# Second pass of a bidirectional DeltaNet layer: which ScalarE and VectorE work may overtake the copies of the triangular inverse

## The chip, the cores and the metric

The kernel runs on one core of a Trainium2 chip. The metric is the device time of one execution in microseconds, on that core. A core has a matmul engine (TensorE, PE in the profile), a vector engine (VectorE, DVE), an activation engine (ScalarE, ACT), a general engine (GpSimd, POOL) and a queue that issues the loads and stores (SyncE, SP). Each works through a list of its own, and they wait for each other by semaphores.

## The reference, cut to what matters

One layer is computed for 128 context tokens and 2048 latent tokens of width 1024: a modulated norm, one input projection, a DeltaNet branch in both directions beside a gated MLP branch, one output projection, and then a squared-ReLU MLP of width 4096 with a final norm. The part that matters here is the DeltaNet scan, in chunks:

```python
decay = where(incl, exp(where(incl, diff, 0.0)), 0.0)      # from the cumulated gates
a_mat = where(strict, einsum(k_beta, k) * decay, 0.0)
sol = triangular_solve(a_mat + eye, rhs, lower=True, unit_diagonal=True)
...
def step(S, xs):
    v_new = u_c - w_c @ S
    o = qd @ S + qk_c @ v_new
    S = S * exp(gl) + kd.T @ v_new
    return S, o
```

It runs once forwards and once backwards over the tokens. The two outputs are added, normed, gated, put through the output projection, added to the input, and normed again for the MLP.

## The kernel before, in words

The program has three stages one after the other: the projections in token blocks (to about 436 us), the two scan passes (about 436 to 1235 us), and the MLP in a seven-product scheme per 2x2 block (from 1237.4 us, the first MLP matmul).

**Units.** The scan works in tiles of 128 tokens. There are 34 units: units 0 to 16 are the forward pass, units 17 to 33 the backward one (`d = 1`), which is called the second pass here. A unit has 17 `prep` steps and 4 `scan` steps, for all four heads at once.

- Step 0 makes the decays: `E = exp(-|g_i - g_j|)`, four ScalarE operations (line 1052) and one exponential (1053), then two masks on GpSimd (`Es`, line 1055, and `E`, line 1057).
- Step 1 makes the matrix: `KK` times beta times `Es` (VectorE, 1067, inside the helper `calm`), its diagonal on GpSimd (1071), its fp16 copy `AH` (ScalarE, 1074) and the first approximate inverse `X = AH * bd2` (VectorE, 1075).
- Step 2 transposes `X` into `Y` (matmuls of line 1081, copy of line 1083) and makes the rest `AL` (VectorE, 1084).
- Steps 3 to 12 are the levels 2, 4, 8, 16, 32: at each the inverse of blocks of twice the size is made from the smaller ones. Each has two steps: matmuls of line 1101 and a masking multiplication on VectorE (`P`, line 1105, the *mask*); then matmuls of lines 1114 and 1116 and two copies on ScalarE (`Y`, line 1117, and `X`, line 1118, the *level copies*).
- Steps 13 and 14 are the last level: matmuls of line 1133 and a ScalarE copy (1134); then matmuls of 1140 and 1142 and two copies, `Y` on VectorE (1143) and `X` on ScalarE (1144). This is the *64-join*.
- Step 15 makes the residual `R` (matmuls of 1150 and 1151, VectorE 1153), step 16 the corrected inverse `T` (ScalarE, 1162).
- The four scan steps: `vt` and the first part of the output from the state (1174, 1166); `vs` and `vn` (1187, 1189); the new state `S`, four VectorE operations (1201); the output (1215 to 1221).

**What fills the matmul engine.** In the second pass the 17 units are filled up with the output of the layer: `o_steps` norms the scan's output (`norm`, 1350 to 1358, ScalarE squares, VectorE sums and products, a power on GpSimd), transposes it and splits it into high and low parts (`trans`, 1371, `oH` 1374 on ScalarE, `oL` 1375 on VectorE), and projects it (`proj`, lines 241 to 243 in the helper `mm3`, then 1394 and 1395). For tiles over 8, `h2_steps` makes the operands of the MLP: squares (868), norm (876, 183, 184), scaling (881), transposes (888, 891), and seven operands `opH`, `opL` (903, 904).

**Order.** Every step has a due time in units of one scan unit. Steps are written out sorted by it, and the place in this order is a priority. The framework then plans each engine's list in a simulated timeline: an instruction whose inputs are there by that timeline may be placed ahead of one that was written earlier but still waits. On the chip the lists are fixed.

Two helpers limit this. `level_done(s)` notes the last instruction written as the latest urgent one of its engine (masks on VectorE, level copies on ScalarE). `calm(f, lag)` writes `f` and forbids each of its instructions to be placed ahead of the latest (`lag` = 0), the last but one (1) or the last but two (2) urgent instruction noted so far on its engine. It adds no wait on a semaphore, only an order within one engine. Before the change it is used, in the second pass, for `KK` (lag 1), for `x = x + tmp` in `proj`, and for the seven operands (`st[5:]`).

The due times in the second pass (`WINDOWS`, last ten values): prep steps of unit i lie from i - 2.63 to i + 0.06, 0.158 apart, so that three units are in work at any time; the scan steps lie at i - 0.03, i + 0.26, i + 0.56 and i + 0.85. The 64-join of unit i + 1 is due at i + 0.664.

Of the kernel before, what the change touches and what calls it, by code (L numbers as in the profile page):

```python
# [12 lines left out]
AF = mybir.ActivationFunctionType  # L13
ALU = mybir.AluOpType
# [7 lines left out]
NT = 17  # L22
NTOK = NT * P
H = 4
# [40 lines left out]
def hybrid_step(  # L65
# [7 lines left out]
    V, A, G, T = nc.vector, nc.scalar, nc.gpsimd, nc.tensor  # L73
# [52 lines left out]
    bd2 = cp.tile([P, P], F16, name="bd2")  # L126
# [21 lines left out]
    def bc4(ap):  # L148
        return ap.unsqueeze(1).to_broadcast([P, 4, P])
# [6 lines left out]
    gcol = cp.tile([P, NT, 8], F32, name="gcol")  # L156
    neg2 = cp.tile([P, NT, 8], F32, name="neg2")
    eglg = cp.tile([P, NT, 8], F32, name="eglg")
    egl = cp.tile([P, NT, 8], F32, name="egl")
# [51 lines left out]
    def here():  # L211
        return len(tc.nc.cur_bb.bb.instructions)
# [82 lines left out]
    with ExitStack() as ph:  # L295
# [17 lines left out]
        for d in range(2):  # L313
            m = p1.tile([P, P], F32, tag=f"mcum{d}", name=f"mcum{d}", bufs=1)
            s = 1 if d == 0 else -1
# [473 lines left out]
        decay = decay_steps()  # L789
        prev = None  # L790
        side = []
        for bi in range(len(BLOCKS)):
# [6 lines left out]
            at = {e: n for n, e in enumerate(order)}  # L799
            tile_of = {}  # L800
            for n, (gi, h) in enumerate(order):
                u = us[n] if bi == 0 and n < 3 else feature_tile(blk, bi, gi, h)
# [157 lines left out]
    with ExitStack() as ph:  # L960
# [8 lines left out]
        def pd():  # L969
            return psd.tile([P, 4, P], F32, tag="d", name="pd", bufs=4)  # L970
# [7 lines left out]
        def f16(tag, bufs=1):  # L978
            return pp.tile([P, 4, P], F16, tag=tag, name=tag, bufs=bufs)

        def q32(tag, bufs=1, pool=None):
            return (pool or dl).tile([P, 4, P], F32, tag=tag, name=tag, bufs=bufs)

        def s32(name):
            return pp.tile([P, 4, P], F32, tag="e", name=name, bufs=NE)
# [16 lines left out]
        def level_done(n):  # L1002

            x = tc.nc.cur_bb.bb.instructions[-1]
            urgent[x.engine].append(x)

        def calm(f, lag=0):

            start = here()
            f()  # L1010
            for x in tc.nc.cur_bb.bb.instructions[start:]:
                if x.engine in urgent and len(urgent[x.engine]) > lag:
                    tc.add_manual_dep(x, urgent[x.engine][-1 - lag].name, mybir.DependencyInfo(
                        mybir.DependencyClass.NoSync, mybir.DependencyReason.DATA), reason="order")

        def unit(t, d):

            u = {}
            sg = 1 if d == 0 else -1

            def col(tab, h):
                return tab[:, t, d * 4 + h : d * 4 + h + 1]

            def quad(p, lhs, rhs):
                for h in range(H):
                    T.matmul(p[:, h, :], lhs[:, h, :], rhs[:, h, :], start=True, stop=True)  # L1026
# [19 lines left out]
            scan = []  # L1046

            @prep.append
            def _():
                e = s32("E")  # L1050
                for h in range(H):
                    A.activation(e[:, h, :], u["gb"][:, h, :], AF.Abs, scale=-1.0, bias=col(gcol, h))
                A.activation(e, e, AF.Exp, scale=-1.0)
                es = s32("Es")
                G.affine_select(out=es, in_=e, pattern=[[0, 4], [-sg, P]], compare_op=ALU.is_gt, fill=0.0,
                                base=0, channel_multiplier=sg)
                G.affine_select(out=e, in_=e, pattern=[[0, 4], [sg, P]], compare_op=ALU.is_ge, fill=0.0,
                                base=0, channel_multiplier=-sg)
                u["Es"], u["E"] = es, e

            @prep.append
            def _():
                a = u["KK"]

                def decayed():
                    for h in range(H):
                        V.scalar_tensor_tensor(out=a[:, h, :], in0=a[:, h, :], scalar=col(beta, h),  # L1067
                                               in1=u["Es"][:, h, :], op0=ALU.mult, op1=ALU.mult)

                calm(decayed, 1) if d else decayed()  # L1070
                G.affine_select(out=a, in_=a, pattern=[[0, 4], [1, P]], compare_op=ALU.not_equal, fill=1.0,
                                base=0, channel_multiplier=-1)
                u["AH"], u["AL"], u["X"] = f16("AH", BA), f16("AL", BA), f16("X", BX)
                A.copy(u["AH"], a)
                V.tensor_tensor(out=u["X"], in0=u["AH"], in1=bc4(bd2), op=ALU.mult)

            @prep.append
            def _():
# [57 lines left out]
            @prep.append  # L1136
            def _():
                p = pd()
                for h in range(H):
                    T.matmul(p[:, h, 0:64], u["X"][:, h, :], pms[64][:, h, rb], start=True, stop=True)  # L1140
                for h in range(H):
                    T.matmul(p[:, h, 64:P], pms[64][:, h, :], u["X"][:, h, ra], start=True, stop=True)
                V.tensor_copy(u["Y"][ra, :, rb], p[ra, :, 0:64])
                A.copy(u["X"][rb, :, ra], p[rb, :, 64:P])

            @prep.append
# [44 lines left out]
            @scan.append  # L1191
            def _():
                s = u["s"]
                p = pd()
                quad(p, u["kt"], u["vs"])
                sn = q32("S", 2)
                if s is None:
                    A.copy(sn, p)
                else:
                    for h in range(H):  # L1200
                        V.scalar_tensor_tensor(out=sn[:, h, :], in0=s[:, h, :], scalar=col(egl, h),
                                               in1=p[:, h, :], op0=ALU.mult, op1=ALU.add)
                u["sn"] = sn

            @scan.append
# [205 lines left out]
        def at(time, fn, kind=None):  # L1411
            events.append((time, len(events), fn, kind))

        def spread(t0, t1, steps, kind):
            for j, st in enumerate(steps):
                at(t0 + (t1 - t0) * (j + 0.5) / len(steps), st, kind)

        def scan_step(i, f):
            def g():
                u = units[i]  # L1420
                if "s" not in u:
                    u["s"] = None if i in (0, NT) else units[i - 1]["sn"] if i not in (1, NT + 1) else u["s0"]
                f()
            return g
# [12 lines left out]
        def noted(name, f):  # L1437

            start = here()
            f()  # L1440
            done[name] = tc.nc.cur_bb.bb.instructions[start:]
# [8 lines left out]
        p2, p3 = WINDOWS[:8], WINDOWS[8:]  # L1450
        for i, u in enumerate(units):
            w = p2 if i <= NT else p3
            at(i - 3 if i > 1 else -12.1, lambda i=i, u=u: noted(("kk", i), u["prep_loads"]))
            at(i - 3 if i > 1 else -11.1, lambda i=i, u=u: after_weights(
                u["qk_load"], (("kk", 1),) if i < 2 else (), (mybir.EngineType.SP,)))
            at(i - 1, lambda i=i, u=u: after_weights(u["scan_loads"], LATER.get(i, ()), (mybir.EngineType.SP,)))
            u["prep"][:2] = [lambda i=i, f=f: after_weights(f, AHEAD_OF.get(i, ()), (mybir.EngineType.Activation,
                                                                                    mybir.EngineType.DVE))
                             for f in u["prep"][:2]]
            n = len(u["prep"])  # L1460
            for j, st in enumerate(u["prep"]):
                at(i - w[0] + (j + 0.5) * (w[0] - w[1]) / n if i or j > 9 else -11.6 if j < 2
                   else 0.2 * j - 8.15, st, "prep")
            spread(i + w[2], i + w[3], [scan_step(i, f) for f in u["scan"]], "chain")
            if i in (0, NT):
                at(i - 1, lambda i=i: state_load(i))
                at(i + w[2] + (w[3] - w[2]) * 0.7, lambda i=i: after(i))
            if i >= NT:
                at(i, lambda u=u: o_loads(u))
                first, second = o_steps(u)  # L1470
                spread(i + p3[4], i + p3[5], first, "fill")
                spread(i + p3[6], i + p3[7], second, "fill")
                if u["t"] > 8:
                    st = h2_steps(u["t"], pj, fraw, w512, fpart, fhalf, lambda u=u: u["x2"])
                    spread(i + p3[8], i + p3[9] + 0.2, st[:5], "fill")
                    spread(i + p3[9] + 0.2, i + p3[9] + 2.1, [lambda f=f: calm(f) for f in st[5:]], None)
        f2 = [f2_steps(t) for t in range(NT)]
        flat = []
# [13 lines left out]
        for j, st in enumerate(flat[:NF]):  # L1492
            g, k = divmod(j, KT + 1)
            if g == 1 and k == KT:
                st = lambda st=st: after_weights(st, AHEAD_OF[0], engines)
            if j == HT * (KT + 1):
                st = lambda st=st: after_weights(st, (("u", 4),), (mybir.EngineType.SP,))
# [457 lines left out]
    for j, t in enumerate(range(8, -1, -1)):  # L1955
        st = h2_steps(t, bank, lambda: w512("junk"), w512)
        p = 10 + 19 * j // 2
# [7 lines left out]
    for p, (o, n, b) in enumerate(seq):  # L1965
        u = units[n]
# [11 lines left out]
        e = p - last  # L1978
# [15 lines left out]
    for m, (n, i, u, q) in enumerate(todo):  # L1994
# [14 lines left out]
        h, lo = sops.pop(m)  # L2009
# [87 lines left out]
```

## Time and profile before

| | |
|---|---|
| median of 3 runs | 2576.61 us (2570.27 to 2578.84) |
| the profiled execution | 2574.76 us, of which the span of instructions is 2573.0 us |
| PE busy | 2536.3 us (99%) |
| DVE busy | 1830.8 us (71%) |
| ACT busy | 1260.1 us (49%) |
| POOL busy | 229.3 us (9%) |
| stretch 520 to 870 us (forward pass) | PE busy 347.70 of 350 us, DVE 245.45, ACT 188.89 |
| stretch 870 to 1215 us (second pass) | PE busy 330.40 of 345 us, DVE 276.22, ACT 224.03 |

Rows of a timeline give start, duration, engine, line, operation, the tiles and, in brackets, how long the engine stood idle before and what ended that. A matmul's duration runs past the start of the next one, since they are pipelined. A row of waits gives who waited for whom, the sum in us, how often, and the longest. A row of windows gives the busy time of the five engines in a stretch, then the granted clock of the matmul engine, the share of the DMA engines and GB/s.

### The profile page before, as it was taken

What the parts mean: (1) busy time and instruction counts of PE and PEld (TensorE: products, weight loads), DVE (VectorE), ACT (ScalarE), POOL (GpSimd) and SP (SyncE); (2) the same over time, 40 slices, a digit from 0 to 9 for tenths busy, and PEclk for the clock granted to TensorE, in tenths of its full rate; (3) what the DMA queues carried; (4) which work ended last, traced back from release to release, by engine and by line L of the source; (5) the groups of instructions that cost most, each with busy time, mean ns of one, the idle gap of its engine ahead of it and who ended that gap; (6) DMA issues with size and microseconds to landing.
All of it is one profiled execution on the core that took longest, in us unless ns stands there. A gap on an engine that the chain in (4) does not pass through costs nothing.

```text
span 2573.0 us, 44472 instructions
## 1 busy us (share of the span) xinstructions
PE 2536.3 (99%) x15268; PEld 2136.7 (83%) x15268; DVE 1830.8 (71%) x3790; ACT 1260.1 (49%) x3119; POOL 229.3 (9%) x448
## 2 busy tenths in 40 slices
PE   9999999999999999999999999999999999999998
PEld 5999999788888788778888888888888887888887
DVE  5867756776676878885678877777675556785875
ACT  4755556555555767763355544444342433243442
POOL 3112212211110111110000000000000000000000
PEclk9999999999999999999999999999999999999999
DMA  8977737744445657785867789665589979776673
GB/s 286 310 215 212 212 114 245 248 160 148 145 155 166 213 190 247 253 280 183 292 199 245 238 281 348 195 180 172 146 272 374 334 263 314 256 258 205 221 264 112
DMA packets 503912, 588.66 MB, mean 229 GB/s; under 512 B 36148, under 2 KB 298588, under 8 KB 500102
## 3 DMA queue, kind: packets, MB, share of 16 engines
q1 hardware_dynamic: 503686, 585.82, 69.7%
q8 instruction: 120, 1.97, 0.3%
q14 instruction: 106, 0.87, 0.1%
HBM read 406.01 MB, written 179.67 MB: 228 GB/s over the span
## 4 chain that ended last, share of the span: by engine, by line
PE 56%; DVE 3%; DMA 3%; ACT 1%; issue 1%; SPq 0%; POOL 0%; POOLq 0%; DVEq 0%; ACTq 0%
PE f L243 16%; PE f L241 16%; PE f L242 16%; PE pd L1026 2%; PE pj L241 1%; PE pj L242 1%; PE pj L243 1%; DMA QK<-qk_d 1%; DMA raw<-in_w_ff_dram 1%; DVE opL L904 0%; DMA kT<-kT_d 0%; DMA h_d<-ev 0%; DVE o L1358 0%; DVE KK L1067 0%; DMA zraw<-z_d 0%
## 5 line engine op out<-in xcount | busy, mean ns | idle before, releaser
L243 PE MATMUL f<-hop,zL 128*128 128x512 f32 (+1 forms) x976 | 377.0, 387 | 1.8 <-DVE zL L1551 1.8
L241 PE MATMUL f<-hop,zH 128*128 128x512 f32 (+1 forms) x976 | 376.9, 387 | 1.2 <-ACT zH L1557 1.2
L242 PE MATMUL f<-hop,zH 128*128 128x512 f32 (+1 forms) x976 | 376.7, 386 | 0.0
L241 PE MATMUL f<-hop,wH 128*128 128x512 f32 x896 | 349.7, 391 | 1.6 <-ACT p L1630 1.6
L242 PE MATMUL f<-hop,wH 128*128 128x512 f32 x896 | 348.7, 389 | 0.0
L243 PE MATMUL f<-hop,wL 128*128 128x512 f32 x896 | 347.3, 389 | 0.0
L1557 ACT CAST zH<-zraw 128x512 fp32r<-128x512 f32 x240 | 146.8, 620 | 295.6 <-DVE zraw L1551 84.2
L243 PEld LDWEIGHTS f<-hop,zL 128*128 128x128 f32 x976 | 183.6, 188 | 39.5 <-DVE zL L1551 3.0
L241 PEld LDWEIGHTS f<-hop,zH 128*128 128x128 f32 x976 | 183.7, 188 | 38.7 <-ACT zH L1557 1.6
L242 PEld LDWEIGHTS f<-hop,zH 128*128 128x128 f32 x976 | 183.7, 188 | 37.7 <-DVE hop L1551 0.3
L1551 DVE TENSOR_TENSOR zL<-zraw,zH 128x512 fp32r<-128x512 f32 x240 | 163.3, 689 | 68.8 <-ACT zH L1557 55.7
L241 PEld LDWEIGHTS f<-hop,wH 128*128 128x128 f32 x896 | 168.2, 188 | 37.3 <-ACT p L1630 3.1
L243 PEld LDWEIGHTS f<-hop,wL 128*128 128x128 f32 x896 | 168.2, 188 | 35.5
L242 PEld LDWEIGHTS f<-hop,wH 128*128 128x128 f32 x896 | 168.3, 188 | 34.6
L241 PE MATMUL pj<-kH,wH 128*128 128x386 f32 (+2 forms) x568 | 190.5, 338 | 1.8 <-ACT junk L601 1.1
L243 PE MATMUL pj<-kH,wL 128*128 128x386 f32 (+2 forms) x568 | 189.7, 335 | 0.0
L242 PE MATMUL pj<-kL,wH 128*128 128x386 f32 (+2 forms) x568 | 189.4, 335 | 0.0
L184 POOL TENSOR_TENSOR r<-rsq,nhalf 128x1 f32<-128x1 f32 (+1 forms) x37 | 23.0, 622 | 1398.1 <-DVE rsq L183 1398.1
L571 DVE SCALAR_TENSOR_TENSOR cv<-pj,vec,cv 128x384 f32<-128x384 f32 (+2 forms) x164 | 87.1, 540 | 53.3 <-ACT cv L568 52.0
L1557 ACT CAST wH<-s 128x512 fp32r<-128x512 f32 x96 | 59.4, 621 | 124.7 <-DVE s L1551 118.2
L241 PEld LDWEIGHTS pj<-kH,wH 128*128 128x128 f32 x568 | 107.1, 189 | 5.3 <-issue 2.1
L202 DVE TENSOR_TENSOR wL<-raw,wH 128x512 fp32r<-128x512 f32 x120 | 81.1, 685 | 38.8 <-ACT wH L201 38.6
(423 smaller groups left out, 5793.6 us busy)
## 6 DMA issues: line engine op xcount, KB each, us to landing
zraw<-z_d SPq DMA_DIRECT2D x212, 256.0 KB
raw<-in_w_ff_dram SPq DMA_DIRECT2D x192, 256.0 KB
hop<-hop_d SPq DMA_DIRECT2D x28, 1024.0 KB
z_d<-c SPq DMA_DIRECT2D x96, 256.0 KB
zraw<-s_d SPq DMA_DIRECT2D x96, 256.0 KB
raw<-in_w_mod_dram SPq DMA_DIRECT2D x80, 256.0 KB
r<-in_w_ff_dram SPq DMA_DIRECT2D x80, 256.0 KB
s_d<-s SPq DMA_DIRECT2D x64, 256.0 KB
```

What stands on the lines that cost most here:

```text
L184: G.tensor_tensor(out=out, in0=t[:np_, :n], in1=nhalf[:np_, :n], op=ALU.pow)
L202: V.tensor_tensor(out=lo, in0=raw, in1=f32(h), op=ALU.subtract)
L241: T.matmul(ps, lh, rh, start=first and i == 0, stop=False, skip_group_check=more)
L242: T.matmul(ps, lh, rl, start=False, stop=False, skip_group_check=more)
L243: T.matmul(ps, ll, rh, start=False, stop=last and i == n - 1, skip_group_check=more)
L571: V.scalar_tensor_tensor(out=cv[:, o : o + m], in0=ps[:, s + sh : s + sh + m], scalar=convw[:, w, j : j + 1], in1=cv[:, o : o + m], op0=AL ...
L1026: T.matmul(p[:, h, :], lhs[:, h, :], rhs[:, h, :], start=True, stop=True)
L1551: V.tensor_tensor(out=out, in0=a, in1=b, op=op)
L1557: A.copy(h, src)
```

## The change

All of it touches the second pass alone.

- The decays (`E`, 1052 and 1053) are tied behind the last but two level copies on ScalarE.
- `AH` and `X` are tied behind the latest level copy and the latest mask.
- `level_done(64)` notes the `Y` copy of the 64-join (VectorE) as urgent; the ScalarE half of the join is not noted.
- The state's update (1201) is tied behind the latest noted VectorE instruction, and the scan step that holds it, with its matmuls, is due 0.12 units later, at i + 0.68, which puts it behind the 64-join of unit i + 1 at i + 0.664 in the written order.
- The first three steps of `o_steps` (`norm`, both `trans`) are tied, and the first five of `h2_steps` (squares, norm, scaling, transposes).

`calm` orders only ScalarE and VectorE instructions; matmuls, GpSimd work and loads inside the tied steps stay as free as before. The number of instructions and their shapes stay the same.

```diff
             def _():
                 e = s32("E")
-                for h in range(H):
-                    A.activation(e[:, h, :], u["gb"][:, h, :], AF.Abs, scale=-1.0, bias=col(gcol, h))
-                A.activation(e, e, AF.Exp, scale=-1.0)
+
+                def decay():
+                    for h in range(H):
+                        A.activation(e[:, h, :], u["gb"][:, h, :], AF.Abs, scale=-1.0, bias=col(gcol, h))
+                    A.activation(e, e, AF.Exp, scale=-1.0)
+
+                calm(decay, 2) if d else decay()
...
-                A.copy(u["AH"], a)
-                V.tensor_tensor(out=u["X"], in0=u["AH"], in1=bc4(bd2), op=ALU.mult)
+                def parts():
+                    A.copy(u["AH"], a)
+                    V.tensor_tensor(out=u["X"], in0=u["AH"], in1=bc4(bd2), op=ALU.mult)
+                calm(parts) if d else parts()
...
                 V.tensor_copy(u["Y"][ra, :, rb], p[ra, :, 0:64])
+                level_done(64)
                 A.copy(u["X"][rb, :, ra], p[rb, :, 64:P])
...
-                    for h in range(H):
-                        V.scalar_tensor_tensor(out=sn[:, h, :], in0=s[:, h, :], scalar=col(egl, h),
-                                               in1=p[:, h, :], op0=ALU.mult, op1=ALU.add)
+                    def update():
+                        for h in range(H):
+                            V.scalar_tensor_tensor(out=sn[:, h, :], in0=s[:, h, :], scalar=col(egl, h),
+                                                   in1=p[:, h, :], op0=ALU.mult, op1=ALU.add)
+                    calm(update) if d else update()
...
-            spread(i + w[2], i + w[3], [scan_step(i, f) for f in u["scan"]], "chain")
+            for j, f in enumerate(u["scan"]):
+                behind_join = 0.12 if j == 2 and i > NT else 0.0
+                at(i + w[2] + (w[3] - w[2]) * (j + 0.5) / 4 + behind_join, scan_step(i, f), "chain")
...
-                spread(i + p3[4], i + p3[5], first, "fill")
+                spread(i + p3[4], i + p3[5], [lambda f=f: calm(f) for f in first], "fill")
...
-                    spread(i + p3[8], i + p3[9] + 0.2, st[:5], "fill")
+                    spread(i + p3[8], i + p3[9] + 0.2, [lambda f=f: calm(f) for f in st[:5]], "fill")
```

## The prediction

> **What bounds the kernel now.** I read the page first, then the two scan passes as windows, then who the matmul engine waited for in the second one, and last the timelines around its longest waits.
>
> ```profile
> PE 2536.3 (99%) x15268; PEld 2136.7 (83%) x15268; DVE 1830.8 (71%) x3790; ACT 1260.1 (49%) x3119; POOL 229.3 (9%) x448
> ```
>
> ```profile
> 520.00:870.00 350.00, 347.70 (x3025) 291.15 (x3025) 245.45 (x679) 188.89 (x515) 41.68 (x56) 1.00 0.50 160
> 870.00:1215.00 345.00, 330.40 (x2923) 275.25 (x2922) 276.22 (x697) 224.03 (x700) 49.37 (x62) 1.00 0.68 229
> ```
>
> PE is the bound everywhere, and the change neither adds nor removes an instruction. What it can gain is PE's idle time in the second pass: 345 - 330.40 = 14.6 us, where the forward pass, on the same chain, has 2.3 us in 350. DVE is busy for 80% of the second pass (276.22 of 345) and ACT for 65%, so both have room, but DVE not much. The waits that make up the 14.6 us:
>
> ```profile
> PE pd L1150 <- DVE Y L1143: 4.9, 7, 1.9
> PE pd L1101 <- ACT Y L1117: 4.2, 7, 1.3
> PE pd L1133 <- ACT Y L1117: 2.0, 4, 0.9
> PE pd L1026 <- ACT X L1118: 1.4, 1, 1.4
> PE pd L1026 <- DVE rsq L183: 1.1, 1, 1.1
> PE pd L1114 <- DVE P L1105: 0.6, 1, 0.6
> ```
>
> All but the rsq line name the copies and masks of the triangular inverse, the very instructions that the change calls urgent. A wait costs a little more than its idle time: matmuls overlap, so an idle gap also loses the overlap. Here a matmul lasts 0.22 us and the next starts 0.05 to 0.06 us later, so I add 0.17 us for each wait that goes.
>
> ```profile
> 1158.83 0.22 PE L1151 MATMUL pd<-Y,AL 128*128 128x128 f16 x1
> 1158.88 0.22 PE L1150 MATMUL pd<-Y,AH 128*128 128x128 f16 x1
> ```
>
> **The change, part by part.** *State's update behind the 64-join.* The seven waits for the join's Y, and what DVE did ahead of the longest:
>
> ```profile
> 1022.47 0.22 PE L1150 MATMUL pd<-Y,AH 128*128 128x128 f16 x1 [0.43 <-DVE Y L1143]
> 1045.20 0.22 PE L1150 MATMUL pd<-Y,AH 128*128 128x128 f16 x1 [0.78 <-DVE Y L1143]
> 1090.97 0.22 PE L1150 MATMUL pd<-Y,AH 128*128 128x128 f16 x1 [0.33 <-DVE Y L1143]
> 1114.13 0.22 PE L1150 MATMUL pd<-Y,AH 128*128 128x128 f16 x1 [0.41 <-DVE Y L1143]
> 1136.64 0.22 PE L1150 MATMUL pd<-Y,AH 128*128 128x128 f16 x1 [0.79 <-DVE Y L1143]
> 1158.77 0.22 PE L1150 MATMUL pd<-Y,AH 128*128 128x128 f16 x1 [1.86 <-DVE Y L1143]
> 1180.69 0.22 PE L1150 MATMUL pd<-Y,AH 128*128 128x128 f16 x1 [0.29 <-DVE Y L1143]
> ```
>
> ```profile
> 1157.05 1.12 DVE L1201 SCALAR_TENSOR_TENSOR S<-S,egl,pd 128x128 f32<-128x128 f32 x4
> 1158.19 0.43 DVE L1143 CAST Y<-pd 64x256 f16<-64x256 f32 x1
> ```
>
> The four S operations stand ahead of Y without a gap in five of the seven; in the one at 1136.64 an oL lies between them, and at 1180.69 Y waited for its own matmuls. S ahead delays Y by 1.14 us (1157.05 to 1158.19). Behind the join it frees five waits whole, 0.43 + 0.78 + 0.33 + 0.41 + 0.79 = 2.74 us and 5 x 0.17, and 1.12 us of the sixth: 4.7 us in all. What is late next is S itself, by one Y copy (0.43 us) and its later matmuls. Its reader comes long after: the S that ended at 1158.17 is used for the vt below, which starts at 1165.11. I cost the delay at nothing under that cover of 7 us; were it gone, S would cost its 1.12 us in each of some 14 units. S also keeps its PSUM tile longer, one of four that the whole chain shares; no row shows what that costs, between nothing and one Y copy for each of 14 units, 6 us. It goes into the returned waits below.
>
> ```profile
> 1165.11 1.12 DVE L1174 SCALAR_TENSOR_TENSOR vt<-pd,neg,vt 128x128 f32<-128x128 f32 x4
> ```
>
> *AH, X and oH behind the level copies.* ACT's list before the wait at 910.61, and the waits of the same kind:
>
> ```profile
> 908.70 0.59 ACT L1189 COPY vn<-pd 128x512 f32<-128x512 f32 x1 [5.55 <-DVE vs L1187]
> 909.18 0.62 ACT L1074 CAST AH<-KK 128x512 f16<-128x512 f32 x1
> 909.70 0.59 ACT L1374 CAST oH<-pm 128x512 fp32r<-128x512 f32 x1
> 910.17 0.39 ACT L1117 CAST Y<-pd 128x256 f16<-128x256 f32 x1
> ```
>
> ```profile
> 910.61 0.28 PE L1133 MATMUL pd<-Y,AH 128*128 128x64 f16 x4 [0.94 <-ACT Y L1117]
> 993.81 0.28 PE L1133 MATMUL pd<-Y,AH 128*128 128x64 f16 x4 [0.26 <-ACT Y L1117]
> 994.85 0.28 PE L1101 MATMUL pd<-Y,AH 128*128 128x64 f16 x4 [0.29 <-ACT Y L1117]
> 1060.99 0.28 PE L1133 MATMUL pd<-Y,AH 128*128 128x64 f16 x4 [0.27 <-ACT Y L1117]
> 1085.35 0.28 PE L1101 MATMUL pd<-Y,AH 128*128 128x64 f16 x4 [0.80 <-ACT Y L1117]
> 1131.02 0.28 PE L1101 MATMUL pd<-Y,AH 128*128 128x64 f16 x4 [1.28 <-ACT Y L1117]
> ```
>
> AH and oH were due after this Y but took its place, 0.52 and 0.47 us from start to start. Both tied, Y starts 0.99 us earlier. At 993.81 and 994.85 the same pair stood ahead, at 1060.99 AH alone: these three go whole, 0.82 us and 3 x 0.17. At 1085.35 and 1131.02 AH stood ahead behind a vn, which stays free: 0.52 us each. Together 0.99 + 1.33 + 1.04 = 3.4 us. The pair of waits at 888 us stays, since oH ran there until Y was ready, and so do those at 885 us, behind work that isn't tied.
>
> *Decays.* Ahead of the 1.4 us wait for X (line 1118) stood the exponential of the decays:
>
> ```profile
> 1067.51 0.63 ACT L1053 ACTIVATE E<-E 128x512 f32<-128x512 f32 x1
> 1068.03 0.37 ACT L1117 CAST Y<-pd 128x256 f16<-128x256 f32 x1
> ```
>
> It delays the copies by 0.52 us, which I count as 0.5. The delay of E costs nothing: this E is that of unit 31, whose X (below) comes 44 us later, with two POOL masks and KK between.
>
> *Output norms and MLP operands.* The wait for the mask P (0.6 us, and 0.17) had the four products of a norm and an opL ahead; 0.7 us goes. Squares and the copies of the transposes were ahead of small waits only; nothing is counted. These steps issue loads (ob, x and the operands' partners) on SP, which the ties don't hold; the tied ACT and DVE work behind them moves by one or two copies, and the matmuls that read oH and oL have other fill work beside them in PE's list. If that cover failed, it would be a wait of 0.3 to 0.7 us (the rows above) for each of 32 transposed halves, up to 20 us; the forward pass, without output work, can't show it.
>
> *The clock.* A long wait has a second price here:
>
> ```profile
> 883.50:886.91 3.41, 2.12 (x29) 1.92 (x29) 3.24 (x10) 2.51 (x10) 0.73 (x1) 1.00 0.42 145
> 1156.54:1159.95 3.41, 1.55 (x20) 1.40 (x20) 2.59 (x7) 0.95 (x2) 0.00 (x0) 1.00 0.83 257
> 1159.95:1163.36 3.41, 3.41 (x15) 2.44 (x14) 1.18 (x3) 1.61 (x8) 0.00 (x0) 0.50 0.65 216
> ```
>
> After 3.41 us in which PE was busy for 1.55 us, the granted clock is 0.50 for the next 3.41 us; after a stretch with 2.12 us it stays at 1.00. The half clock loses 1.7 us. With 1.12 us of the wait at 1158.77 gone, PE would be busy for some 2.7 us there, so the 1.7 us go too. The Trainium skill (TensorE: Matmul & The Clock Gate, Part 1: The HAM clock gate (the "warmup" mystery)) says that the clock halves after an idle window of about 3.4 us. The window's length agrees with this trace, but its condition is stricter than what the trace shows, for here 1.86 us of idle time within the window sufficed. By the page's rule the half clock would have another cause and would stay, and my sum would be 1.7 us smaller.
>
> *The sum.* 4.7 + 3.4 + 0.5 + 0.7 + 1.7 = 11.0 us freed. Against it stand new waits, because every tied instruction comes later and each engine's list is laid out anew. Between 0 and all 11 us I take 5 us, nearest to the row of the Y copy: 0.43 us, once in each of about 13 units. The net is -6 us: 2568.8 us against the profiled execution's 2574.76. The median of the runs shown lies 1.85 us above that execution, so I forecast 2570.5 us. The MLP behind it takes the shift whole, since its own start waits only for this pass, and PE is 99% busy after it.
>
> **The rivals.** *All of it arrives, and more.* The wait for rsq (1.1 us) also follows a late join, and prompt copies free PSUM tiles earlier. Nothing is handed back: 2576.6 - 11 = 2565.5 us, and with all 14.6 us idle, their overlaps (22 x 0.17 = 3.7 us) and the clock gone 2556.5 us, the floor. For it speaks that the forward pass runs this chain with 2.3 us idle; against it, that output work on DVE fills the second pass to 80%.
>
> *The waits only change their name.* The ties bind the planner's simulated list, and the chip's late instructions are others: tmp, vn, KK, the R of the rsq line. All 11 us come back as waits for these: 2574 to 2579 us, no change. For it speaks that vn stood ahead twice already.
>
> *AH comes too late for its own unit.* AH waits behind two pairs of level copies, X behind a mask, and then X's transposition is what PE waits for. In units 21 to 33 the time from the end of X to the matmuls of line 1081 is between 1.2 and 4.8 us. A thin case, unit 31 (1.4 us), and a wide one, unit 32 (4.3 us):
>
> ```profile
> 1111.48 0.41 DVE L1075 TENSOR_TENSOR X<-AH,bd 128x512 f16<-128x512 f16 x1
> 1113.32 0.40 PE L1081 MATMUL pd<-ident,X 128*128 128x128 f16 x4
> ...
> 1130.73 0.43 DVE L1075 TENSOR_TENSOR X<-AH,bd 128x512 f16<-128x512 f16 x1 [0.57 <-ACT AH L1074]
> ...
> 1135.46 0.39 PE L1081 MATMUL pd<-ident,X 128*128 128x128 f16 x4
> ```
>
> The covers of the 13 units sum to 41.5 us. Delayed by 5 us each, they would lose 13 x 5 - 41.5 = 23.5 us, and the time is 2576.6 - 11 + 23.5 = 2589 us, slower. The point from which it loses is about 3.8 us of delay, where the four thin units (27, 28, 31, 33) and the middling ones together pay 11 us. Against it: in the case above the tie costs AH four copies at 0.27 us, about 1.1 us, less than the thinnest cover. It needs copies whose own matmuls come late.
>
> **How the numbers follow.** Forecast (2566.5 to 2573.5): 0.48. All of it and more: 0.17. Only renamed: 0.22. AH too late: 0.13. What a measurement can tell from no change is 0.3%, 7.7 us, so faster means below 2568.9 us: the second case whole, and the lower third or so of the forecast, 0.36. Slower means above 2584.3 us, nearly all of the last case, 0.12. The rest is 0.52. The range from 2560 to 2582 us reaches from half the way between full gain and floor to the mild end of the late AH, and leaves out about 0.15.
>
> **What would show it.** Right: waits for Y of line 1143 in the second pass under 1.5 us in sum, those for Y of line 1117 under 4 us, S behind the join's Y in DVE's list, no half clock near 1160 us, and the MLP's first matmul 5 to 8 us earlier than 1237.4. Wrong: PE's idle time in the pass again near 14 us with other names (tmp, vn, X of line 1075, oL), a longer stretch of waits at line 1081, or a half clock that stays.

## The result, and the profile after

The changed kernel takes 2603.64 us (median of 6 runs) against 2576.94 us (6 runs): a ratio of 1.0116, 95% interval 1.0100 to 1.0132. It is 27 us slower, and outside the forecast range. The time is lost in the second pass. Windows from 870 us to the first MLP matmul, of before and then of after:

```profile
870.00:1237.40 367.40, 352.80 (x3025) 293.80 (x3024) 292.16 (x727) 230.32 (x716) 50.37 (x63) 1.00 0.67 223
```

```profile
870.00:1268.30 398.30, 362.98 (x3010) 303.92 (x3009) 292.51 (x720) 226.48 (x719) 50.45 (x64) 0.98 0.61 204
```

The MLP starts 30.9 us later. PE is idle for 35.3 us instead of 14.6, and busy for 10 us more with the same matmuls. Half of these 10 us is the clock: it was halved for 13.7 us instead of 3.4, which loses 5.1 us more. The rest fits the overlaps lost at 25 more waits (48 over 0.15 us, 23 before): at the prediction's 0.17 us each, an estimate, 4.3 us. DVE's and ACT's work is nearly unchanged. Behind it, the MLP itself is 3 us shorter (2573.0 - 1237.4 against 2600.8 - 1268.3). PE's waits in the second pass of after:

```profile
PE pd L1148 <- ACT P L1142: 8.6, 9, 1.7
PE pd L1159 <- ACT X L1126: 5.4, 7, 1.0
PE pd L1089 <- DVE X L1081: 4.9, 2, 3.8
PE pj L1384 <- DVE o L1371: 3.8, 3, 2.4
PE pd L1109 <- ACT Y L1125: 1.6, 4, 0.8
PE pd L1141 <- ACT Y L1125: 1.5, 2, 1.0
```

In after's numbering, 1142 is the copy P of the 64-level (1134 before), 1126 the level copy X (1118), 1081 the first inverse X (1075), 1371 the products of the output norm (1358), 1125 the level copy Y (1117). The waits that the change aimed at did go: those for the join's Y fell from 4.9 to 0.4 us, those for the level copy Y from 6.2 to 3.1. Others took their place, with more time than they had. PE's list around two of them, at unit 29, first the stretch between join and residual in before (the residual, line 1150, starts at 1114.13), then after:

```profile
1111.85 0.47 PE L241 MATMUL pm<-wH,oH 128*128 128x512 f32 x1
1112.16 0.39 PE L242 MATMUL pm<-wL,oH 128*128 128x512 f32 x1
1112.39 0.40 PE L243 MATMUL pm<-wH,oL 128*128 128x512 f32 x1
1112.62 0.40 PE L241 MATMUL pm<-wH,oH 128*128 128x512 f32 x1
1112.86 0.39 PE L242 MATMUL pm<-wL,oH 128*128 128x512 f32 x1
1113.09 0.40 PE L243 MATMUL pm<-wH,oL 128*128 128x512 f32 x1
```

```profile
1131.97 0.28 PE L1148 MATMUL pd<-P,X 128*128 128x64 f16 x4 [1.19 <-ACT P L1142]
1132.08 0.28 PE L1150 MATMUL pd<-X,P 128*128 128x64 f16 x4
1132.19 1.14 PE L1026 MATMUL pd<-vs,kt 128*128 128x128 f32 x8
1133.17 0.28 PE L1122 MATMUL pd<-P,X 128*128 128x64 f16 x4
1133.29 0.28 PE L1124 MATMUL pd<-X,P 128*128 128x64 f16 x4
1133.40 0.39 PE L1089 MATMUL pd<-ident,X 128*128 128x128 f16 x4
1134.75 0.22 PE L1159 MATMUL pd<-Y,AH 128*128 128x128 f16 x1 [0.96 <-ACT X L1126]
```

Between the 64-join (1148, 1150) and the residual (1159) no filling matmul stands here in after. Over units 21 to 32 there are 1.2 matmuls of the projection (lines 241 to 243) on average in this place, where before there were 5.5; between the 64-level and the join there are now 12.5 (6.5 before). The average hides how they stand: before, there were six in each of the two places in 11 of the 12 units; after, 36 stand together in units 23, 26, 28 and 30, and seven of the other eight units have none in either place. The filling matmuls have changed places in PE's list, and where they are gone, PE waits out the copies.

What moved them shows at the output norm. Before, its squares (ACT, line 1350) start as soon as the output o (DVE, 1220) is there:

```profile
1069.92 0.69 DVE L1220 TENSOR_TENSOR o<-o,pd 128x512 f32<-128x512 f32 x1 [0.36 <-PE pd L1026]
...
1070.65 0.34 ACT L1350 ACTIVATE junk<-o 128x128 bf16<-128x128 f32 x1
```

After, for unit 28 (o is line 1233, the squares 1363):

```profile
1136.97 0.68 DVE L1233 TENSOR_TENSOR o<-o,pd 128x512 f32<-128x512 f32 x1
...
1148.05 0.40 ACT L1363 ACTIVATE junk<-o 128x128 bf16<-128x128 f32 x1
```

On average over units 21 to 31 the squares start 0.05 us after o before the change and 12.1 us after it now, and the last oL is done 16.3 us after o before, 28.4 us now.

### The profile page after: what moved, and what is told of

Read it like the earlier page. It is cut to its first block, busy times and chain, and to the rows that moved or that the text cites. A ratio compares the mean times of both kernels' runs of the same rounds, so it can differ in the third digit from the quotient of the medians.

```text
span 2600.8 us, 44424 instructions
## 1 busy us (share of the span) xinstructions
PE 2545.9 (98%) x15268; PEld 2147.3 (83%) x15268; DVE 1831.4 (70%) x3790; ACT 1253.9 (48%) x3119; POOL 228.4 (9%) x448
## 4 chain that ended last, share of the span: by engine, by line
PE 88%; DMA 4%; ACT 3%; DVE 3%; issue 1%; SPq 0%; POOL 0%; POOLq 0%; ACTq 0%
PE f L241 16%; PE f L243 16%; PE f L242 16%; PE pj L241 7%; PE pj L243 7%; PE pj L242 7%; PE pd L1026 5%; PE pm L241 2%; PE pm L243 2%; PE pm L242 2%; PE pt L625 1%; DMA raw<-in_w_mod_dram 1%; PE pt L584 1%; DMA raw<-in_w_ff_dram 1%; PE pd L1109 1%
```

## The experiments

Each stands against runs of the kernel before on the same chip. A "part alone" is the kernel before with that part of the change. Ratios have 95% intervals.

**The join part alone:** `level_done(64)`, `calm(update)`, and the scan step 0.12 later.

> The kernel before with the join part alone: the 64-join's Y noted as urgent, the state's update tied behind it, its scan step due 0.12 units later. If the output part (norm, transposes tied) is what costs the 27 us, this alone gives what was priced for it, 3 to 6 us under before (2571 to 2574), with the waits for the join's Y (6.0 us in seven places before) nearly gone. If the later state itself is the cost (its PSUM tile, the chain from state to state), it is 5 to 25 us over before, with new waits at S or at vt.

1.0015 (1.0006 to 1.0024). The waits for the join's Y are gone, but ACT's copies P and Y, and tmp (DVE) are waited for instead: 4.6 us in eight places for tmp behind oL, 6.0 us with the overlaps. The half clock comes twice instead of once.

**AH and X alone:** `calm(parts) if d else parts()`.

> The kernel before with AH and X alone tied behind the level copies and masks. Theory of the output part: 0 to 4 us under before. Rival (AH too late for its own unit): 10 us or more over before, with waits of the matmuls that transpose X (5.3 us in two places after the whole change, none before).

1.0001 (0.9992 to 1.0011). Neither the gain of 3.4 us nor the rival's loss; no wait for X of line 1075.

**The output part alone:** `[lambda f=f: calm(f) for f in first]`.

> The kernel before with the first three output steps alone tied (norm, both transposes). Theory of the output part: 10 us or more over before (2587 to 2605), with waits for the 64-level copy P on ScalarE (10.5 us in ten places after the whole change, 0.4 before) behind squares of the norm, and transposes that wait for the norm's products. Rival (the parts only hurt together, or AH is the cause): within 4 us of before.

1.0217 (1.0200 to 1.0235), 56 us. Twice the loss of the whole change, from one part, and beyond the range expected. The expected sign is missed: P is waited for 3.1 us, the join's Y 16.2 us.

**The whole change without it:**

> The whole change without the tie on the first three output steps. Theory of the output part: at most 8 us over before (under 2585), the waits for P and for the norm's products gone. Rival (AH too late, or the state's step): stays over 2590.

1.0064 (1.0047 to 1.0081), 17 us, 2590.56 us: the theory's bound is missed and the rival's just met, so a second part loses too. AH and X alone and the join alone, which the rival named, don't cost that; what is left are the decays and the MLP's operands.

**The decays alone:** `calm(decay, 2) if d else decay()`.

> The kernel before with the decays alone tied behind the last but two level copies. Under both theories it is hidden: E was ready some 40 us before its use. Within 4 us of before; if it is 8 us or more over before, holding ScalarE work back bunches the queue whatever the work is, and the output part is not special.

0.9978 (0.9968 to 0.9988): 5.7 us faster, where 0.5 us was forecast. Here ScalarE work that can wait may be held back. Why it gains so much more than forecast stays open; the half clock, one stretch before, is gone too.

**The MLP's operands alone:** `[lambda f=f: calm(f) for f in st[:5]]`.

> The kernel before with the first five steps of the MLP's operands alone tied. Theory that only work which feeds the filling matmuls hurts: within 5 us of before, since these steps feed nothing but four transposes and the store of operands. Rival (whatever is held back bunches): 8 us or more over before, in units 25 to 32 alone.

1.0068 (1.0053 to 1.0083), 17 us. The theory that only work which feeds the filling matmuls hurts seems to fall here; how it feeds them is shown further down.

**The output part split.** Norm alone: `[lambda f=first[0]: calm(f)] + first[1:]`.

> Of the output part only the norm tied (squares on ScalarE, sums and products on VectorE), the two transposes free. If the norm's length is the cause (eight ScalarE and seven VectorE pieces held back, then the transposes, oH, oL and the projection wait in turn): at least two thirds of the 56 us of the whole output part, 2610 or more. If the copies oH and oL are the cause: under 2590.

1.0215 (1.0198 to 1.0232): the norm is the whole of it. Transposes alone: `first[:1] + [lambda f=f: calm(f) for f in first[1:]]`.

> Of the output part only the two transposes' copies tied (oH on ScalarE, oL on VectorE), the norm free. If the copies are the cause: 2600 or more, with filling matmuls of lines 241 to 243 waiting for oH and oL. If the norm is the cause: under 2590.

1.0017 (1.0007 to 1.0026). With the norm alone tied the squares start 14.9 us after o on average and are spread over 5.0 us (1.7 before). PE's longest waits in that kernel:

```profile
PE pd L1150 <- DVE Y L1143: 16.2, 11, 2.7
PE pj L243 <- DVE oL L1375: 8.6, 3, 5.1
PE pd L1101 <- ACT Y L1117: 5.7, 12, 1.0
```

The theory formed from this: a tied step can't pass copies that were written before it, so it runs no earlier than its *written* place. The norm is written at i + 1.41 units, the step that makes its input at i + 0.85. A unit lasts 22.3 us, so the tie holds it back by about 0.56 x 22.3 = 12 us, near the 12.1 and 14.9 us seen. The planner had run it half a unit ahead of where it was written.

**The norm tied, written at i + 0.90.**

```diff
-                spread(i + p3[4], i + p3[5], first, "fill")
+                at(i + 0.9, lambda f=first[0]: calm(f), "fill")
+                for j, f in enumerate(first[1:]):
+                    at(i + 1.5 + 0.28 / 3 * j, f, "fill")
```

> The norm alone tied, but written 0.51 units earlier, at i + 0.90, just behind the scan step that makes its input; the transposes stay where they were. With the norm tied at i + 1.41 the squares start 14.9 us after the output is there (0.05 us before the change). Theory of the written place (a tied step can't run ahead of copies written before it, so it waits for its written place): the squares start 0 to 4 us after the output and the time is within 6 us of before. Rival (the order between squares and copies itself, or bunching on ScalarE, is the cost): still over 2600.

1.0015 (1.0003 to 1.0027). ACT's timeline there has the squares at o again:

```profile
1073.32 0.31 ACT L1350 ACTIVATE junk<-o 128x128 bf16<-128x128 f32 x1 [0.75 <-DVE o L1220]
```

The same tie, 51 us less: the written place is the cause, not the order as such. The projection's matmuls between 64-level, join and residual stand as before in all 12 units from 21 to 32.

**The projection half a unit later,** free and with the norm tied at its old place: the last four values of `WINDOWS` from `1.66, 2.66, 3.17, 3.71` to `2.16, 3.16, 3.67, 4.21`.

> Control: the kernel before, nothing tied, with the projection and the MLP's operands written 0.5 units later. The output work ends half a unit (11 us) later at most; 2570 to 2592.

> The norm alone tied at its place i + 1.41, and the projection and the MLP's operands 0.5 units later. Theory that the late norm costs because the filling matmuls planned behind it get their operands too late: the control's time plus 0 to 12 us, so most of the 55 us is gone. Rival (the held work bunches on ScalarE and VectorE and delays the triangular chain wherever the fill stands): 40 us or more over the control.

The control is at 1.0018 (1.0007 to 1.0029), with the norm tied it is at 1.0046 (1.0032 to 1.0060). The norm is nearly as late as without this edit (13.2 us after o, against 14.9), ACT and DVE hold the same work back, but 55 us have shrunk to 11, 8 over the control. In PE's list the projection's matmuls stand as before in eight of the 12 units, and no unit is without them; with the norm alone tied, eight of the 12 had none in either place. So most of the loss is fill that is planned too close behind a late norm. The order within ACT and DVE costs little by itself.

**The whole change without the join part:**

> The whole change without the join part (the state's update free, its step at its old place). Alone the join part cost 4.8 us. If the parts add up, this is about 2599, 5 under the whole change. If the join part repairs part of what the late norm does (18 us of waits for the join's Y behind the state's update with the norm alone tied, 0.6 us after the whole change), it is 2612 to 2630.

1.0176 (1.0155 to 1.0197), 2618 us. Where the fill fails, the join waits for Y behind S:

```profile
PE pd L1158 <- DVE Y L1151: 18.3, 12, 2.4
PE pd L1089 <- DVE X L1081: 8.4, 4, 2.7
```

In the whole change these waits are 0.4 and 4.9 us. The join part, which costs 4 us alone, is worth some 15 us in this company, so the parts can't be added.

**The MLP's operands tied, written 0.45 units earlier:** `spread(i + p3[8] - 0.45, i + p3[9] - 0.25, ...)`.

> The first five steps of the MLP's operands alone tied, but written 0.45 units earlier, from i + 2.72, just behind the projection's last step at i + 2.60. Theory of the written place: within 6 us of before (tied at the old place, it was 17 us over). Rival (holding this work back costs wherever it is written): 12 us or more over.

1.0079 (1.0064 to 1.0094). For this part the theory of the written place fails in this form: the time stays, only the waits change. The projection's matmuls stand as in before again, in all 12 units. But seven transposes now wait for the load of ob, together 12.9 us:

```profile
PE pm L1371 <- DMA ob<-ob_d: 7.8, 4, 2.2
PE pj L1371 <- DMA ob<-ob_d: 5.1, 3, 2.6
```

**The whole change, norm at i + 0.90 and the operands 0.45 earlier:**

> The whole change, every tie kept, with the norm written at i + 0.90 and the first five steps of the MLP's operands from i + 2.72. Theory of the written place: the 27 us shrink to within 8 us of before. Rival (the ties themselves, in sum, cost): stays 15 us or more over.

1.0014 (1.0004 to 1.0024): every tie kept, and 24 of the 27 us are gone. The ties on output and operands aren't free even so: on the same chip this kernel takes 2576.40 us, and without these two ties (next) 2564.02 us.

**Decays, AH and X, and the join part together,** output and operands free.

> The three parts that were priced as gains, together: decays, AH and X, and the join part; output and MLP operands free. Alone they measured -0.22%, +0.01% and +0.15%. If they add up: 2570 to 2577. If the prediction's price for join, AH and clock holds once nothing else is tied: 2565 to 2568. If the join part costs more in company: over 2580.

0.9957 (0.9942 to 0.9972): 2564.02 us against 2573.82, faster than both kernels, and just under the range that the prediction's price gave. Its stretch to the MLP and PE's longest waits in it:

```profile
870.00:1230.70 360.70, 353.26 (x3040) 295.25 (x3039) 292.23 (x733) 235.54 (x728) 55.67 (x68) 1.00 0.69 230
```

```profile
PE pd L1109 <- ACT Y L1125: 1.8, 3, 0.8
PE pj L241 <- DVE tmp L1407: 1.5, 2, 0.7
PE pd L1148 <- ACT P L1142: 1.1, 2, 0.6
```

PE is idle for 7.4 us instead of 14.6, and the half clock near 1160 us is gone.

**Decays, AH and X:**

> The two ScalarE parts alone, decays and AH and X. As a sum of the single runs 2566 to 2574, and the candidate for a version that beats both kernels; over 2577 if they disturb each other.

0.9978 (0.9967 to 0.9988): the sum of the two, half of the gain. The join part, which costs 4 us alone, brings the other half here: without it the join's Y is waited for 6.8 us, with it 0.6. That it gains because ACT's copies are prompt here (2.2 to 2.5 us of waits for the level copy Y, 8.0 with the join part alone) is likely, but wasn't tested by itself.

**The operands part split.** With it tied, in units 20 to 27 alone the power of the *output's* norm runs 9 to 16 us after its squares (0.5 to 2.7 before). First, norm2 alone left free:

> The first five steps of the MLP's operands tied as in only_h2, but norm2 (the sum and the product before the power on GpSimd) free. Theory of the power: the output norm's power comes within 4 us of its squares again, and the time is within 6 us of before. Rival (squares, scaling and transposes held back are the cost, or norm2 is late anyway because its squares are tied): 2586 or more.

1.0059 (1.0038 to 1.0081): no help, and the power is still 7 to 14 us late; as the rival said, norm2 is late when its squares are. Then norm2 alone tied, `calm` for `j == 1` only:

> Of the MLP's operands norm2 alone tied. Theory of the power: two small VectorE instructions a tile, eight tiles, cost 10 us or more (2584 or more), with the output norm's power 8 us or more after its squares. Rival: within 5 us of before.

1.0063 (1.0038 to 1.0088): these two small instructions a tile cost 15 us. DVE, GpSimd and ACT there, for the output norm whose squares ended at 1062.73:

```profile
1062.54 0.19 ACT L1350 ACTIVATION_READ_ACCUMULATOR junk<-o 128x1 f32 x1
```

```profile
1072.86 0.15 DVE L876 TENSOR_TENSOR ss<-ss 128x1 f32<-128x1 f32 x1
...
1074.58 0.15 DVE L183 TENSOR_SCALAR rsq<-ss 128x1 f32<-128x1 f32 x1
1074.64 0.16 DVE L183 TENSOR_SCALAR rsq<-r 128x4 f32<-128x4 f32 x1
```

```profile
1075.34 0.56 POOL L184 TENSOR_TENSOR r<-rsq,nhalf 128x1 f32<-128x1 f32 x1
1075.86 1.01 POOL L184 TENSOR_TENSOR rr<-rsq,nhalf 128x4 f32<-128x4 f32 x1
```

The output norm's product (from r) and its power (rr) stand right behind those of the MLP's norm (from ss, and r) on both engines, twelve microseconds after the squares. So the tied operands do reach the filling matmuls, by way of the output norm behind them: the last oL is done 23.0 us after o (16.3 before), and between 64-join and residual stand 2.3 projection matmuls on average (5.5 before). With the operands written 0.45 units earlier, the power was back within 5 us of its squares and the fill in its place, so the loss there, with its waits for ob, is another one; its cause stays open. Why the lists have that order stays open: the MLP's norm is written just before it (for the tile two units older, at 26.39 against 26.41), and both take the same two `rsq` buffers. A buffer of its own for each was not tried.

## Why the prediction was wrong

- **Which waits go: right.** Waits for the join's Y, forecast under 1.5 us, are 0.4; for the level copy Y, under 4, are 3.1; S stands behind the join's Y in DVE's list; the half clock near 1160 us is gone. The four terms for join, AH, decays and clock, 4.7 + 3.4 + 0.5 + 1.7 = 10.3 us, are close to what the three parts gave together (9.8 us; 7 to 15 by the interval). One at a time they did not: +3.9 (join), +0.3 (AH) and -5.7 us (decays), so it is in part luck that the sum agrees.
- **The step that failed: "output norms and MLP operands", costed at nothing under other fill work.** It said that tied work "moves by one or two copies" and priced the failure of the cover at 20 us at most. The norm moved by 12 us, because a tie counts from the written place and the planner had run it half a unit ahead of that. The norm alone cost 55 us, the operands 17. The row that gave it away was in the trace of before: the squares started 0.05 us after o, while their written place lay among copies due half a unit later.
- **The mis-sized term: 5 us of returned waits.** It was taken from one Y copy per unit. Measured, PE's idle time rose by 20.7 us net although 6 us and more of the old waits went, and the half clock took three stretches of 3.4 to 6.8 us instead of one, which lost another 5 us.
- **The state's delay, costed at nothing.** The first readers of S are the matmuls at 1163.46 us in before, not vt at 1165.11, so the cover was 5.3 us and not 7; it held. The price that the prediction left open, a PSUM tile kept longer, can be seen in after: two matmuls of line 1026 that read vn and QK, not S, wait 1.5 us for the update of S, and line 1159 waits 5.4 us for a level copy X that it doesn't read. Both look like waits for a free tile; they are absent where the three gaining parts stand alone, and no run tested them.
- **The rivals.** AH too late for its own unit: waits for that X came to 4.9 us in two places, but behind four S operations in DVE's list, and AH and X alone cost nothing; the loss is not its work. Renamed waits came true, but with about three times the time, and mostly under names that were not forecast (the copy P, the level copy X, the norm's products). The forecast direction, faster, holds only without the output and operand parts.
- **The cover "matmuls that read oH and oL have other fill work beside them" was wrong in kind.** oH and oL *are* what the fill needs: when they come 12 us late, the fill itself moves in PE's list, as the 36 matmuls in one place show.

## What to carry to other kernels

Before tying an instruction behind others in a planned order, compare when it runs now with where it is written: the tie takes away all of that lead, here half a unit, not the length of the instructions ahead. Move the written place first, then tie (the same tie cost 55 us at i + 1.41 and 4 us at i + 0.90), and measure: for the MLP's operands the earlier place did not help. And tie only work whose result nobody awaits soon; what feeds the filling of the bounding engine, even through a small sum on another engine, is not such work.

## What the runs showed of the hardware

In these runs the half clock follows a stretch in which PE was busy for less than about half of 3.41 us. In after:

```profile
1138.73:1142.14 3.41, 0.98 (x22) 0.77 (x19) 1.65 (x7) 3.02 (x11) 0.10 (x1) 1.00 0.80 280
```

```profile
1142.14:1145.55 3.41, 3.30 (x21) 3.18 (x22) 2.36 (x8) 1.91 (x8) 0.00 (x0) 0.50 0.42 158
```

Over the second passes of all kernels here, 59 half-clock stretches followed windows busy for 0.60 of the time or less. Of the windows that kept the full clock none was busy for less than 0.47; between 0.47 and 0.60 both happened. Above, one wait of 2.38 us does it, but shorter ones together are enough: the window before the half clock at 889.55 us of after was busy for 1.42 of 3.41 us, and its longest idle piece was 1.17 us (the others 0.55 and 0.27). No idle window is needed.
